# Hybrid attention and retention trunk: one transfer per row tile, rotation read from PSUM, queries and keys written to their final tiles, outputs kept in the gate tiles

## The chip, the core and the metric

The kernel runs on one core of one Trainium2 chip. A core has a matrix engine (TensorE, PE in the profile; PEld is its weight load), VectorE (DVE), ScalarE (ACT) and GpSimd (POOL), which work side by side, each through its own program, and wait for each other by semaphores. SyncE (SP) issues the transfers here; they run on 16 DMA engines. Working memory is SBUF, 128 partitions wide; matrix products land in PSUM. The metric is the device time of one execution in microseconds (us). The kernel before took 2116.13 us (median of three runs, 2115.45 to 2116.34).

## What is computed

Two layers over 2048 tokens of width 1024, then a last norm. Each layer norms its input, projects it to eight sections, runs attention over half of the width and retention over the other half, gates both, projects back and adds:

```python
def hybrid_layer(x, norm_gain, w_in, w_out, rel_bias, cos, sin):
    b, s, _ = x.shape
    hn = rms_norm(x, norm_gain)
    proj = hn @ w_in.astype(hn.dtype)
    cuts = list(np.cumsum(SPLIT_WIDTHS)[:-1])
    aq, ak, av, ag, rq, rk, rv, rg = jnp.split(proj, cuts, axis=-1)
...
    y = jnp.concatenate([ya * jax.nn.silu(ag.astype(jnp.float32)),
                         yr * jax.nn.silu(rg.astype(jnp.float32))], axis=-1).astype(x.dtype)
    return x + y @ w_out.astype(x.dtype)

def apply_rotary(t, cos, sin):
    t1, t2 = jnp.split(t, 2, axis=-1)
...
    return jnp.concatenate([t1 * c - t2 * s, t1 * s + t2 * c], axis=-1)
```

Attention has 8 heads of 64; each chunk of 64 tokens sees itself and the 8 chunks before it, with a learned bias by distance. Retention has 4 heads of 128: its queries and keys are turned by `apply_rotary`, a decaying state goes from chunk to chunk, and each head's output is normed. All inputs are float32.

## The kernel before

Every float32 operand of a matrix product is held as two fp16 parts, an upper one and a rest, and each product is made of three (upper by upper, rest by upper, upper by rest). A rest costs an operation of its own: ACT copies the upper part, and DVE subtracts it from the source.

The normed input lies transposed in `hTh` and `hTl` (L215), one pair for each stripe of 512 tokens. It gets there by row tiles of 128 tokens: `rows_hi` and `rows_lo` (L225 to L233) write the two halves, and `transpose_rows` (L235) turns each with a DMA transpose of its own. A row pair takes its two tiles from the tags `sc` and `pq`, which attention uses too.

For each layer, a loop goes over four groups `s` (two attention heads and one retention head each) and, within, over four stripes `n`. A stripe's dense work is 24 rounds of eight matmuls:

- `dense_T` (L608): sections j = 0 to 3 are attention queries, attention keys, retention queries and retention keys, three rounds each, into a PSUM tile of which there are two. `evacuate` (L627) then copies. The queries go through ACT (L631) and DVE (L634) into `qq`, and four transfers put both halves of both heads on all partitions of `st.q`. The keys go through L645 and L648 into `kk`, and four transfers place them in `st.k`. The retention sections are copied to SBUF (L662), two transfers swap the partition halves into `swp`, and DVE multiplies by the cosine table, multiplies the swapped copy by the sine table, and adds (L670). ACT and DVE then split the result (L673, L676), and keys are transposed to token order.
- `dense_V` (L738): for four token tiles a, the values of both heads, the retention values `rv` and the gate `gt`. ACT makes the upper parts and the gate's tanh (L760 to L763), DVE the rests (L766 to L770). The gate's pool has five buffers.

While PE does these rounds for one stripe, the attention and retention of the stripe before run between them. `attention` (L778) has eight units of a token tile and a head, three rounds each: PE makes the scores S (L800, L801), DVE adds the bias and takes the maximum (L804), ACT the exponential and its upper part (L807, L809), POOL the rest (L810), a DMA transpose turns the weights into `pT` (L812), and a unit later PE multiplies them with the values (L820 to L822). `out_` (L824) scales by the row sum and the gate into `ya`, and one transfer per token tile writes `y_d` in DRAM. `retention` (L866) makes dT (DVE mask L875, ACT L860, DVE rest L864), then the output and the state's update; `fin` (L911) scales by the norm and the gate into `yr`, and a second transfer goes to `y_d`.

After a layer's four groups, `wout` takes the 16 token tiles: it loads `y_d`, scales it into fp16 halves, transposes them (`y_turn`, L954; into the buffers of `tabc`, `tabs`, `qq` and `swp`) and multiplies by the output weights; `residual` adds the input and makes the next layer's rows.

PE, ACT, DVE and POOL run in the order in which the program is written. `later(k, fn)` puts a step k rounds off, and `tick` (once a round) issues what is due. The order of SP's transfers is chosen by a scheduler, and by hand only in the prologue. `push` and `pull` spread the preparation of weights over the rounds. The trigonometric tables are made by `tables` (L83) for each stripe, written to `tab_d` in eight transfers and loaded per stripe by `tab_load` (L613).

## Time and profile before

| | us |
|---|---|
| median of three runs | 2116.13 |
| the profiled execution's span | 2120.7 |
| PE busy in it | 2014.2 |
| DVE busy | 1341.8 |
| ACT busy | 1136.9 |
| POOL busy | 432.8 |

The profile is one execution, its span 4.6 us above the median. It shows each engine's busy time and what ended each idle stretch. In a group's row stand line, engine, operation, output and inputs by name, shapes and number, then busy time, mean nanoseconds of one, and the idle time ahead with what ended it. In the timeline a row has its start and length in us; brackets hold the idle time just before it and its releaser. Rows of SPq are the issue of a transfer, not its flight. A row of waits has the total, the number and the longest. In the transfers' rows the last number is the median from issue to landing.

The execution has a prologue up to about 90 us (norms of the first tokens, weights, tables, the first dense rounds), the 16 stripe rounds of layer 0 up to about 890, the output projection of layer 0 up to about 1110, the same for layer 1, and the last projection from about 1930.

### The profile page before, as it was taken

Reading aid. Unit: us, or ns where it says so; the run is one execution under the profiler, and the core shown is the slowest. Engines: PE = TensorE matmul, PEld = TensorE weight load, DVE = VectorE, ACT = ScalarE, POOL = GpSimd, SP = SyncE. Lnnn points to the kernel's source line nnn. Section 1 sums busy time; section 2 is a strip of 40 time slices with the busy share of each in tenths; the row PEclk is TensorE's granted clock in tenths of the full one; section 3 lists DMA queues with packets and bytes.
Section 4 is the critical chain, followed back from the end, with each engine's and each line's share of the span. In section 5 each row is a group of like instructions: output and inputs, shape, how many; then the busy total and the mean of one; then the engine's idle time right before and its main releaser. Section 6 shows DMA issues by size and latency. Waiting matters only on the chain.

```text
span 2120.7 us, 39351 instructions
## 1 busy us (share of the span) xinstructions
PE 2014.2 (95%) x14014; PEld 1052.9 (50%) x14014; DVE 1341.8 (63%) x4031; ACT 1136.9 (54%) x2522; POOL 432.8 (20%) x509
## 2 busy tenths in 40 slices
PE   6788999999999999988999999999999999998998
PEld 4334455555555555444444555555555555554543
DVE  7667666666656666566654666566666566666643
ACT  7455565556565554554544546554655665445432
POOL 1112221222122212221000222222222222222200
PEclk9989999999999999999999999999999999999999
DMA  8757675557476765689865556655666866648864
GB/s 247 173 111 162 138 157 119 115 110 156 109 166 133 157 164 100 120 189 254 219 179 123 119 100 135 130 119 100 140 129 123 172 152 157 124 101 176 217 193 127
DMA packets 645702, 313.63 MB, mean 148 GB/s; under 512 B 459233, under 2 KB 602081, under 8 KB 645505
## 3 DMA queue, kind: packets, MB, share of 16 engines
q1 hardware_dynamic: 645504, 311.12, 66.4%
q8 instruction: 109, 1.79, 0.4%
q14 instruction: 89, 0.72, 0.1%
HBM read 123.26 MB, written 41.98 MB: 78 GB/s over the span
## 4 chain that ended last, share of the span: by engine, by line
PE 50%; DMA 8%; DVE 5%; ACT 5%; issue 1%; SPq 1%; POOL 0%; POOLq 0%; DVEq 0%; ACTq 0%
PE dT L731 16%; PE dV L752 15%; PE dO L1093 12%; DMA pT<-pq 3%; PE r L856 2%; PE S L800 2%; PE S L801 2%; DVE sc L804 1%; DMA toep<-rel_d 1%; DMA swp<-rot 1%; PE o L820 1%; ACT pq L809 1%; PE o L821 1%; PE o L822 1%; ACT sc L807 1%
## 5 line engine op out<-in xcount | busy, mean ns | idle before, releaser
L807 ACT ACTIVATE sc<-sc,mq,cT 128x640 f32<-128x640 f32 (+4 forms) x256 | 218.4, 853 | 657.3 <-DVE mq L806 341.5
L810 POOL TENSOR_TENSOR pq<-sc,pq 128x640 f16<-128x640 f32 (+4 forms) x256 | 322.6, 1260 | 1201.7 <-ACT pq L809 610.3
L731 PE MATMUL dT<-hTh,whT 128*128 128x512 f16 x1008 | 350.2, 383 | 13.4 <-DMA hTh<-hTl 9.8
L752 PE MATMUL dV<-whV,hTh 128*128 128x512 f16 x1024 | 355.3, 383 | 4.1 <-DVE gt L770 4.1
L752 PE MATMUL dV<-wlV,hTh 128*128 128x512 f16 x1024 | 353.8, 381 | 0.0
L752 PE MATMUL dV<-whV,hTl 128*128 128x512 f16 x1024 | 353.7, 381 | 0.0
L731 PE MATMUL dT<-hTh,wlT 128*128 128x512 f16 x1008 | 347.0, 379 | 0.0
L731 PE MATMUL dT<-hTl,whT 128*128 128x512 f16 x1008 | 346.8, 379 | 0.0
L752 PEld LDWEIGHTS <-hTh 128*128 128x128 f16 x2048 | 197.5, 99 | 222.9 <-issue 8.2
L731 PEld LDWEIGHTS <-whT 128*128 128x128 f16 x2016 | 192.9, 98 | 225.8 <-issue 23.1
L804 DVE CUSTOM_DVE_ANT_0 sc<-S,bias 128x640 f32<-128x640 f32 (+4 forms) x256 | 188.6, 737 | 79.9 <-PE S L801 69.0
L1093 PE MATMUL dO<-whO,yhy 128*128 128x512 f16 x512 | 195.0, 381 | 1.1 <-DMA yhy<-rhy 1.1
L1093 PE MATMUL dO<-whO,yly 128*128 128x512 f16 x512 | 194.8, 381 | 1.1 <-DMA yly<-rly 1.1
L1093 PE MATMUL dO<-wlO,yhy 128*128 128x512 f16 x512 | 194.6, 380 | 0.0
L809 ACT ACTIVATE pq<-sc 128x640 f16<-128x640 f32 (+4 forms) x256 | 171.5, 670 | 12.5 <-DMA pT<-pq 4.6
L1093 PEld LDWEIGHTS <-yhy 128*128 128x128 f16 x1024 | 100.0, 98 | 116.7 <-DMA yhy<-rhy 1.9
L752 PEld LDWEIGHTS <-hTl 128*128 128x128 f16 x1024 | 99.5, 98 | 110.5 <-issue 2.6
L731 PEld LDWEIGHTS <-wlT 128*128 128x128 f16 x1008 | 97.6, 98 | 109.0 <-issue 1.8
L800 PE MATMUL S<-k,q 128*128 128x128 f16 (+3 forms) x592 | 143.7, 269 | 5.7 <-DVE mq L804 5.6
L820 PE MATMUL o<-v,pT 128*128 128x65 f16 x1120 | 130.2, 194 | 14.6 <-DMA pT<-pq 14.6
L820 PEld LDWEIGHTS <-pT 128*128 128x128 f16 x1120 | 105.6, 97 | 52.5 <-DMA pT<-pq 24.4
L801 PE MATMUL S<-k,q 128*128 128x128 f16 (+3 forms) x592 | 131.2, 270 | 0.0
(350 smaller groups left out, 3354.4 us busy)
## 6 DMA issues: line engine op xcount, KB each, us to landing
q<-qq SPq DMA_DIRECT2D x128, 128.0 KB, 2.5
yyy<-y_d SPq DMA_DIRECT2D x32, 512.0 KB, 4.6
stT<-in_w_in_dram SPq DMA_DIRECT2D x27, 512.0 KB, 5.0
stV<-in_w_in_dram SPq DMA_DIRECT2D x26, 512.0 KB, 4.5
k<-kk SPq DMA_DIRECT2D x128, 64.0 KB, 2.1
swp<-rot SPq DMA_DIRECT2D x64, 128.0 KB, 2.6
tabc<-tab SPq DMA_DIRECT2D x32, 256.0 KB, 2.7
tabs<-tab SPq DMA_DIRECT2D x32, 256.0 KB, 2.8
```

Source lines behind the costliest of these rows:

```text
L731: pe.matmul(ps, w_[:, j, kt, :], h_[:, kt, :], start=(m == 0), stop=(m == 23))
L752: pe.matmul(ps, h_[:, kt, a * P:(a + 1) * P], w_[:, kt, :], start=(m == 0), stop=(m == 23))
L800: pe.matmul(o, st.q[:, hx, 0, cs], k_, start=True, stop=False)
L801: pe.matmul(o, st.q[:, hx, 1, cs], k_, start=False, stop=True)
L804: dve.tensor_tensor_reduce(out=v, in0=S[:, 0:w], in1=g.bias[hx][:, 640 - w:640], scale=1.0, scalar=-3.0e38, op0=ALU.add, op1=ALU.max, accu ...
L807: act.activation(v, v, AF.Exp, bias=m[:, 0:1], scale=g.c[:, 0:1])
L809: act.activation(pq[:, 0:w], v, AF.Copy)
L810: pool.tensor_tensor(pq[:, w:2 * w], v, pq[:, 0:w], op=ALU.subtract)
L820: pe.matmul(o[:, 0:65], u.p[:, b, :], v_[:, 0:65], start=(b == 0), stop=False)
L821: pe.matmul(o[:, 0:64], u.p[:, b, :], v_[:, 65:129], start=False, stop=False)
L856: pe.matmul(out_, w_, m_, start=(i == 0), stop=(i + 1 == len(pairs)))
L1093: pe.matmul(ps, h_[:, kt, :], w_[:, kt, :], start=(m == 0), stop=(m == 23))
```

## The change

- The two fp16 halves of a row tile lie side by side in one tile, and one transpose turns both into one tile `hT`. The last token tile of `wout` keeps two transposes.
- Scores and weights of an attention unit share one tile `spq` (two buffers), as do row pairs and the scratch of the first tables.
- Tables are written in four transfers, without a negated sine, and loaded with one.
- Queries: ACT and DVE write each head's half straight into `st.q`, and two transfers copy it to the other partitions. Keys: ACT and DVE write `st.k` in place, the rest onto the opposite partitions, with no transfer.
- Rotation: DVE reads the PSUM tile itself, once times cosine and twice, by halves of 64 partitions and onto the opposite half, times plus or minus sine, then adds. There is no copy to SBUF and no swap transfer. The PSUM tile is read until one round after the first product. The steps follow one round apart, and the key's token transpose keeps its distance.
- The three outputs of a token tile are written over the gate they are multiplied with; when the third is there (`finished`), one transfer writes them to `y_d`.
- `y_turn` uses the buffers of `tab` and of the rotation's scratch, tag `qk`.

The order of PE's and POOL's instructions stays the same. The DMA issues on SP fall from 1297 to 795.

```diff
-    tab_d = [dp.tile([2, P, 512], F32, tag=f"tab{n}", name=f"tab{n}") for n in range(NS)]
+    tab_d = [dp.tile([P, 2, 512], F32, tag=f"tab{n}", name=f"tab{n}") for n in range(NS)]
...
-        dve.tensor_scalar(ang, r, -1.0, None, op0=ALU.mult)
...
+        cs_ = wk[:, 512:1024].rearrange("p (a c) -> p a c", a=2)
+        for h in range(2):
+            for hf in range(2):
+                sp.dma_start(tab_d[n][h * 64:h * 64 + 64, :, hf * 256:hf * 256 + 256], cs_[hf * 64:hf * 64 + 64])
...
     def hT_of(l, n):
         if (l, n) not in hT:
-            hT[l, n] = (hp.tile([P, KT, 512], F16, tag="hTh", name=f"hTh{l}_{n}"),
-                        hp.tile([P, KT, 512], F16, tag="hTl", name=f"hTl{l}_{n}"))
+            h_ = hp.tile([P, 2 * KT, 512], F16, tag="hT", name=f"hT{l}_{n}")
+            hT[l, n] = (h_[:, 0:KT], h_[:, KT:2 * KT], h_)
         return hT[l, n]
 
+    def halves_of(rows):
+        return rows[:, 0:D], rows[:, D:2 * D], rows
+
     def row_pair(nm):
-        return (b2.tile([P, 1280], F16, tag="sc", name=f"rh{nm}")[:, 0:D],
-                b2.tile([P, 1280], F16, tag="pq", name=f"rl{nm}")[:, 0:D])
+        return halves_of(b2.tile([P, 2560], F16, tag="spq", name=f"rw{nm}")[:, 0:2 * D])
...
-    def transpose_rows(rows, dh, dl):
-        sp.dma_start_transpose(out=dh, in_=rows[0])
-        sp.dma_start_transpose(out=dl, in_=rows[1])
+    def transpose_rows(rows, dst):
+        sp.dma_start_transpose(out=dst, in_=rows[2])
...
-        st.tabc = b1.tile([P, 512], F32, tag="tabc", name=f"tabc{nm}")
-        st.tabs = b1.tile([P, 512], F32, tag="tabs", name=f"tabs{nm}")
+        st.tab = b1.tile([P, 2, 512], F32, tag="tab", name=f"tab{nm}")
         def tab_load():
             while n not in tab_done:
                 pull(1)
-            sp.dma_start(st.tabc, tab_d[n][0])
-            sp.dma_start(st.tabs, tab_d[n][1])
+            sp.dma_start(st.tab, tab_d[n])
...
         def evacuate(j, ps):
             if j == 0:
                 st.q = b2.tile([P, 2, 2, 512], F16, tag="q", name=f"q{nm}")
-                qq = b1.tile([P, 2, 512], F16, tag="qq", name=f"qq{nm}")
-                act.activation(qq[:, 0, :], ps, AF.Copy, scale=2.0 ** -16)
+                for hx in range(2):
+                    hs = slice(hx * 64, hx * 64 + 64)
+                    act.activation(st.q[hs, hx, 0], ps[hs], AF.Copy, scale=2.0 ** -16)
 
                 def q_rest():
-                    dve.scalar_tensor_tensor(out=qq[:, 1, :], in0=ps, scalar=2.0 ** -16, in1=qq[:, 0, :], op0=ALU.mult,
-                                             op1=ALU.subtract)
                     for hx in range(2):
-                        for half in range(2):
-                            sp.dma_start(st.q[half * 64:half * 64 + 64, hx], qq[hx * 64:hx * 64 + 64])
+                        hs, os = slice(hx * 64, hx * 64 + 64), slice(64 - hx * 64, 128 - hx * 64)
+                        dve.scalar_tensor_tensor(out=st.q[hs, hx, 1], in0=ps[hs], scalar=2.0 ** -16, in1=st.q[hs, hx, 0],
+                                                 op0=ALU.mult, op1=ALU.subtract)
+                        sp.dma_start(st.q[os, hx], st.q[hs, hx])
 
                 soon(q_rest)
             elif j == 1:
                 st.k = b3.tile([P, 2, 512], F16, tag="k", name=f"k{nm}")
-                kk = b1.tile([P, 2, 512], F16, tag="swp", name=f"kk{nm}")
-                kh, kl = kk[:, 0, :], kk[:, 1, :]
-                act.activation(kh, ps, AF.Copy, scale=2.0 ** -16)
+                for hx in range(2):
+                    hs = slice(hx * 64, hx * 64 + 64)
+                    act.activation(st.k[hs, hx], ps[hs], AF.Copy, scale=2.0 ** -16)
 
                 def k_rest():
-                    dve.scalar_tensor_tensor(out=kl, in0=ps, scalar=2.0 ** -16, in1=kh, op0=ALU.mult, op1=ALU.subtract)
-                    sp.dma_start(st.k[0:64, 0, :], kh[0:64, :])
-                    sp.dma_start(st.k[64:128, 1, :], kh[64:128, :])
-                    sp.dma_start(st.k[64:128, 0, :], kl[0:64, :])
-                    sp.dma_start(st.k[0:64, 1, :], kl[64:128, :])
+                    for hx in range(2):
+                        hs, os = slice(hx * 64, hx * 64 + 64), slice(64 - hx * 64, 128 - hx * 64)
+                        dve.scalar_tensor_tensor(out=st.k[os, hx], in0=ps[hs], scalar=2.0 ** -16, in1=st.k[hs, hx],
+                                                 op0=ALU.mult, op1=ALU.subtract)
 
                 soon(k_rest)
             else:
...
+                rot = b2.tile([P, 5 - j, 512], F16, tag=f"rot{j}", name=f"rot{nm}_{j}")
                 if j == 2:
                     st.rq = rot
-                    swap()
+                    st.tmp = b1.tile([P, 2, 2, 512], F16, tag="qk", name=f"tmp{nm}")
                     if first:
                         later(1, tab_load)
                 else:
                     st.rk = rot
-                    later(8 if first else 2, swap)
+                f32 = lambda t_: t_.rearrange("p a c -> p (a c)").bitcast(F32)
+                own = f32(rot[:, 1:3]) if j == 2 else f32(st.tmp[:, 0])
+                other = f32(st.tmp[:, 1])
+
+                def cosine():
+                    dve.scalar_tensor_tensor(out=own, in0=ps, scalar=2.0 ** -16, in1=st.tab[:, 0], op0=ALU.mult,
+                                             op1=ALU.mult)
+
+                def sine(half):
+                    i_, o_ = slice((1 - half) * 64, (2 - half) * 64), slice(half * 64, half * 64 + 64)
+                    dve.scalar_tensor_tensor(out=other[o_], in0=ps[i_], scalar=(half * 2 - 1) * 2.0 ** -16, in1=st.tab[i_, 1],
+                                             op0=ALU.mult, op1=ALU.mult)
+
+                def tokens():
+                    st.kt = b1.tile([P, KT, P], F16, tag="ktok", name=f"kt{nm}")
+                    sp.dma_start_transpose(out=st.kt, in_=rot.rearrange("p a c -> p (a c)"))
+
+                d = 2 * j if first else 1
+                later(d, cosine)
+                later(d, lambda: sine(0))
+                later(d + 1, lambda: sine(1))
+                later(d + 2, lambda: dve.tensor_tensor(own, own, other, op=ALU.add))
+                later(d + 3, lambda: act.activation(rot[:, 0], own, AF.Copy))
+                later(d + 4, lambda: dve.tensor_tensor(rot[:, 1], own, rot[:, 0], op=ALU.subtract))
+                if j == 2:
+                    later(d + 5, lambda: act.activation(rot[:, 2], rot[:, 0], AF.Copy, scale=2.0 ** -11))
+                else:
+                    later(d + 5 if first else d + 12, tokens)
...
-        ya = {}
+        left = [3] * 4
+
+        def finished(a):
+            left[a] -= 1
+            if left[a] == 0:
+                t = 4 * n + a
+                sp.dma_start(y_d[t].rearrange("p (a s c) -> p a s c", a=2, c=P)[:, :, s],
+                             st.g[a].rearrange("p (a c) -> p a c", a=2))
...
-            v = b2.tile([P, 640], F32, tag="sc", name=f"sc{u.nm}")[:, 0:w]
+            spq = b2.tile([P, 2560], F16, tag="spq", name=f"spq{u.nm}")
+            v, pq = spq[:, 0:1280].bitcast(F32)[:, 0:w], spq[:, 1280:2560]
             m = b2.tile([P, 1], F32, tag="mq", name=f"mq{u.nm}")
             dve.tensor_tensor_reduce(out=v, in0=S[:, 0:w], in1=g.bias[hx][:, 640 - w:640], scale=1.0, scalar=-3.0e38,
                                      op0=ALU.add, op1=ALU.max, accum_out=m)
             dve.tensor_scalar(m, m, g.nc[:, 0:1], LN_PSC, op0=ALU.mult, op1=ALU.add)
             act.activation(v, v, AF.Exp, bias=m[:, 0:1], scale=g.c[:, 0:1])
-            pq = b2.tile([P, 1280], F16, tag="pq", name=f"pq{u.nm}")
             act.activation(pq[:, 0:w], v, AF.Copy)
             pool.tensor_tensor(pq[:, w:2 * w], v, pq[:, 0:w], op=ALU.subtract)
...
-                if u.hx == 0:
-                    ya[u.a] = b2.tile([P, P], F32, tag="ya", name=f"ya{u.nm}")
-                y = ya[u.a]
-                vs = slice(u.hx * 64, u.hx * 64 + 64)
-                dve.scalar_tensor_tensor(out=y[:, vs], in0=o[:, 0:64], scalar=rl[:, 0:1], in1=st.g[u.a][:, vs],
-                                         op0=ALU.mult, op1=ALU.mult)
-                if u.hx == 1:
-                    sp.dma_start(y_d[t][:, s * P:(s + 1) * P], y)
+                y = st.g[u.a][:, u.hx * 64:u.hx * 64 + 64]
+                dve.scalar_tensor_tensor(out=y, in0=o[:, 0:64], scalar=rl[:, 0:1], in1=y, op0=ALU.mult, op1=ALU.mult)
+                finished(u.a)
...
             def fin(t=t, a=a, r2=r2, ss=ss, nm=nm):
-                y = b1.tile([P, P], F32, tag="yr", name=f"yr{nm}")
-                dve.scalar_tensor_tensor(out=y, in0=r2[:, 0:P], scalar=ss[:, 0:1], in1=st.g[a][:, P:256],
-                                         op0=ALU.mult, op1=ALU.mult)
-                sp.dma_start(y_d[t][:, 512 + s * P:512 + (s + 1) * P], y)
+                y = st.g[a][:, P:256]
+                dve.scalar_tensor_tensor(out=y, in0=r2[:, 0:P], scalar=ss[:, 0:1], in1=y, op0=ALU.mult, op1=ALU.mult)
+                finished(a)
...
     def y_turn(u):
         if u.t + 1 == NT:
             u.h, u.lo = (b2.tile([P, 10, P], F16, tag="pT", name=f"y{c}{u.nm}")[:, 0:KT, :] for c in "hl")
+            sp.dma_start_transpose(out=u.h, in_=u.rows[0])
+            sp.dma_start_transpose(out=u.lo, in_=u.rows[1])
         else:
-            u.h = b1.tile([P, KT, P], F16, tag=("tabc", "qq")[u.t % 2], name=f"yh{u.nm}")
-            u.lo = b1.tile([P, KT, P], F16, tag=("tabs", "swp")[u.t % 2], name=f"yl{u.nm}")
-        transpose_rows(u.rows, u.h, u.lo)
+            yT = b1.tile([P, 2 * KT, P], F16, tag=("tab", "qk")[u.t % 2], name=f"yT{u.nm}")
+            u.h, u.lo = yT[:, 0:KT], yT[:, KT:2 * KT]
+            transpose_rows(u.rows, yT)
...
```

More of the change, by code (lines that the diff above doesn't have):

```diff
@@ L83, in tables @@
     def tables(n, wk):
-        ang, k, r, k2 = wk
+        ang, k, k2, r = (wk[:, i * 256:(i + 1) * 256] for i in range(4))
         pi = k2.bitcast(I32)
@@ L266, in hi @@
         def hi(self):
-            if self.rows:
-                self.rw = (self.rows[:, 0:D], self.rows[:, D:2 * D])
+            if self.rows is not None:
+                self.rw = halves_of(self.rows)
                 act.activation(self.rw[0], self.x, AF.Copy)
@@ L274, in lo @@
         def lo(self):
-            if self.rows:
+            if self.rows is not None:
                 dve.tensor_tensor(self.rw[1], self.x, self.rw[0], op=ALU.subtract)
@@ L987, in mul @@
         def mul():
-            u.x = xt if on_pe or rows else psS.tile([P, D], F32, tag="S", name=f"xn{nm}")
+            u.x = xt if on_pe or rows is not None else psS.tile([P, D], F32, tag="S", name=f"xn{nm}")
             dve.scalar_tensor_tensor(out=u.x, in0=xt, scalar=u.rs[:, 0:1], in1=gains[l].b, op0=ALU.mult, op1=ALU.mult)
@@ L999, in upper @@
             else:
-                u.rows = rows or row_pair(nm)
+                u.rows = halves_of(rows) if rows is not None else row_pair(nm)
                 rows_hi(u.rows, u.x)
@@ L1180, in dma @@
         def dma(k):
-            transpose_rows(us[k].rows, *us[k].h)
+            transpose_rows(us[k].rows, us[k].h[2])
         us = []
@@ L1261, in hybrid_trunk @@
     sp.dma_start(invf_sb, invf)
-    t0 = tables(0, [gp.tile([P, 256], F32, tag="gt", name=f"wk{i}") for i in range(4)])
+    t0 = tables(0, b2.tile([P, 2560], F16, tag="spq", name="wk").bitcast(F32)[:, 0:1024])
     go_on(t0)
@@ L1328, in V_un @@
         next(vu[0])
-    t1 = tables(1, [xs0[1][:, i * 256:(i + 1) * 256] for i in range(4)])
+    t1 = tables(1, xs0[1])
     steps = {"d": lambda: go_on(d0), "t": lambda: go_on(t0), "u": lambda: go_on(t1), "r": lambda: go_on(rl_),
@@ L1380, in hybrid_trunk @@
                     push(norms_from_input(range(4 * n + 4, 4 * n + 8), late[0:4] if n == 1 else None,
-                                          tables(n + 1, [xs0[n + 1][:, i * 256:(i + 1) * 256] for i in range(4)])), 21)
+                                          tables(n + 1, xs0[n + 1])), 21)
                 if (l, s, n) == (0, 1, 1):
```

69 lines of the change are left out of this document (15 added, 54 removed).

## Prediction

> **What bounds the kernel now.** I read the page's head first, then the busy time stage by stage, then what TensorE (PE) waits for, last the timeline around the longest stalls.
>
> ```profile
> span 2120.7 us, 39351 instructions
> PE 2014.2 (95%) x14014; PEld 1052.9 (50%) x14014; DVE 1341.8 (63%) x4031; ACT 1136.9 (54%) x2522; POOL 432.8 (20%) x509
> 45.00:90.00 45.00, 35.19 (x160) 15.63 (x158) 29.35 (x70) 23.49 (x52) 3.35 (x10) 0.89 0.79 180
> 90.00:215.00 125.00, 102.43 (x664) 51.46 (x663) 84.95 (x235) 66.14 (x143) 27.00 (x32) 0.91 0.66 139
> 300.00:865.00 565.00, 556.84 (x4127) 296.68 (x4126) 366.83 (x1183) 316.34 (x748) 135.49 (x153) 1.00 0.63 133
> 865.00:1010.00 145.00, 126.84 (x851) 64.45 (x850) 90.48 (x253) 76.16 (x146) 27.44 (x28) 0.96 0.89 199
> 1112.00:1890.00 778.00, 767.09 (x5565) 405.80 (x5564) 492.78 (x1551) 427.12 (x1008) 176.27 (x202) 1.00 0.62 129
> 1890.00:2000.00 110.00, 103.01 (x759) 54.12 (x756) 75.06 (x216) 59.70 (x119) 26.66 (x27) 0.98 0.79 182
> ```
>
> PE is the bound: 2014.2 of 2120.7 us. The change leaves its instructions and their order as they are, so all that can be gained is idle time, 106.5 us, and time lost to a lower clock. The rows by stage (length, then busy time of PE, PE's loads, DVE, ACT and POOL, then granted clock) place the idle time: 9.8 us in 45 to 90, 22.6 in 90 to 215, 18.2 in 865 to 1010, 7.0 in 1890 to 2000. The two long steady stretches hold 8.2 and 10.9 in 1343 us; there a shorter wait can bring almost nothing.
>
> ```profile
> PE r L856 <- DVE dT L864: 20.5, 16, 5.1
> PE S L800 <- DVE mq L804: 5.6, 2, 2.9
> DVE rot L670 <- DMA swp<-rot: 60.1, 26, 6.2
> 106.76 0.69 DVE L670 TENSOR_TENSOR rot<-rot,tabc 128x512 f32<-128x512 f32 x1 [2.90 <-DMA swp<-rot]
> 110.43 0.29 PE L856 MATMUL r<-rv,dT 128*128 128x128 f16 x1 [5.07 <-DVE dT L864]
> 729.72 0.68 DVE L670 TENSOR_TENSOR raw<-raw,tabc 128x512 f32<-128x512 f32 x1
> 730.65 0.23 PE L856 MATMUL r<-rv,dT 128*128 128x128 f16 x1 [1.51 <-DVE dT L864]
> ```
>
> A row of waits gives total, number and longest. DVE stands 60.1 us for swap transfers of the rotation, PE only 20.5 for DVE's rest of dT. The two touch where a rotation multiply stands just ahead of that rest in DVE's program order: at 106.76 behind a swap wait, at 729.72 as plain work.
>
> **The change part by part.**
>
> *Row transposes, prologue.* PE's longest stall:
>
> ```profile
> 63.69 1.22 DVE L276 TENSOR_TENSOR hTl<-hTl,hTl 128x1024 f16<-128x1024 f32 x1
> 64.24 3.23 SPq L237 DMA_TRANSPOSE hTl<-hTh  x1
> 72.67 1.56 SPq L236 DMA_TRANSPOSE hTh<-hTl  x1
> 74.32 3.10 SPq L237 DMA_TRANSPOSE hTl<-hTl  x1
> 78.61 3.57 PE L731 MATMUL dT<-hTh,whT 128*128 128x512 f16 x8 [9.81 <-DMA hTh<-hTl]
> 145.24 1.89 PE L731 MATMUL dT<-hTh,whT 128*128 128x512 f16 x8
> 209.96 3.57 PE L731 MATMUL dT<-hTh,whT 128*128 128x512 f16 x8 [3.62 <-DMA hTh<-rhn]
> pT<-pq SPq DMA_TRANSPOSE x256, 3.4
> yhy<-rhy SPq DMA_TRANSPOSE x32, 3.2
> ```
>
> The rows are ready when DVE ends at 64.91, yet SP sends their second half only at 74.32, because the queue ahead is full (two transposes a tile, two swaps, x loads). With one transpose a tile and no swaps, SP is free by then; DVE's own added work (below, 2.8 us) makes the rows ready at about 67.7. A transpose of 16 blocks is not in the trace: 8 blocks land in 3.2 us and 10 in 3.4, so by that slope 16 take 4.0; bounds are 3.2 (no slower) and 6.4 (two of 8 in a row). Landing at 71.7, and PE is there at 68.80: a stall of 2.9 instead of 9.81, **−6.9**. After both DMA stalls here the first eight matmuls took 3.57 us against 1.89, so such a stall costs 1.7 more. I keep that cost here and drop it at 209.96, where one transfer for two and fewer issues ahead should end most of the 3.62: **−3 −1.7**.
>
> By the Trainium skill, "TensorE: Matmul & The Clock Gate", "Why this matters for your kernels", PE gaps over about 3 us bring the clock down; both rows agree, and by that rule the prologue's dip goes if its stall ends below 3.
>
> *Rotation.* Per stripe and group (32 of them) two evacuations and four swap transfers go, and each rotation's four DVE operations become five.
>
> ```profile
> L634 DVE SCALAR_TENSOR_TENSOR qq<-dT,qq 128x512 f16<-128x512 f32 x32 | 21.9, 683 | 13.2 <-ACT qq L631 13.2
> L670 DVE TENSOR_TENSOR rot<-rot,tabc 128x512 f32<-128x512 f32 x32 | 27.9, 871 | 68.3 <-DMA swp<-rot 60.1 <-DMA y_d<-yr 8.1
> L631 ACT ACTIVATE qq<-dT 128x512 f16<-128x512 f32 x32 | 18.8, 587 | 9.8 <-PE dT L731 9.5 <-PE dT L712 0.3
> 1204.86 0.28 DVE L864 SCALAR_TENSOR_TENSOR dT<-dT,r 128x128 f16<-128x128 f16 x1
> 1205.98 0.22 PE L856 MATMUL r<-rv,dT 128*128 128x128 f16 x1
> ```
>
> Halves of 64 partitions have the same 512 elements a partition, so I price each at 0.683, as L634, which reads PSUM as they do; bounds: half of that (fewer partitions) and 0.871. Queries and keys add one such operation each, so DVE gets 4 × 0.683 = 2.7 us a stripe, 88 us in all, against the 60.1 of swap waits that go. ACT stays even: two halves more, two evacuations fewer. What was late behind a swap goes: in 90 to 215 the 5.07 and some 2 us of the smaller stalls, **−7**. In the steady stretches, at stalls like 730.65, the multiply stood ahead of the rest and now comes three rounds earlier. Of the 20.5 us of PE's waits on that rest, six such places hold 0.6 to 1.5 each: **−6**. The cover fails at the retention unit in q's round: its rest ends 0.84 us before PE asks (1205.14 to 1205.98), while DVE now has one operation of 0.68 more ahead of it and may wait 0.59 for ACT's second half. That lacks 0.4; in about half of the stripes the slack is several us instead. Bounds 0 and 32 × 1.3 = 42; I take **+5**. The PSUM tile is held one round longer, within the three rounds until PE needs it: nothing.
>
> The Trainium skill, "VectorE: DVE Perf Modes", "Two Vector instructions with no wait between them", speaks against the change: an instruction whose start quadrant differs from its predecessor's is held until all earlier ones have finished. No row of before has such halves. At an estimated 0.08 us each (the overlap of neighbouring rows here) and some 11 holds a stripe it would be 28 us more of DVE, and by it the sum would end about 3 us higher.
>
> *Queries, keys, tables.* Six q and k transfers a stripe and one table load go from SP; the key transfers (2.1 us to landing) aren't what PE waits for, so beside SP's room this is worth nothing.
>
> *One tile for scores and weights.* DVE's next-but-one reduction now waits for the transpose's landing, not ACT's copy alone.
>
> ```profile
> 592.10 1.25 SPq L812 DMA_TRANSPOSE pT<-pq  x1
> 597.91 0.81 DVE L804 CUSTOM_DVE_ANT_0 sc<-S,bias 128x640 f32<-128x640 f32 x1
> ```
>
> Issue 592.10 plus 3.4 is 595.5, 2.4 before that reduction: a little only in the slow transfers, **+1** (bounds 0 and 21: one transfer in twelve, of 256, late by 1 us).
>
> *Outputs in gate tiles.* The gate tile is free only when its transfer has landed. The last piece written and its transfer now, and ACT's next write:
>
> ```profile
> 1242.97 0.28 DVE L832 SCALAR_TENSOR_TENSOR ya<-o,rl,gt 128x64 f32<-128x64 f32 x1
> 1243.28 0.32 SPq L835 DMA_DIRECT2D y_d<-ya  x1
> 1245.21 0.47 ACT L761 ACTIVATE gt<-dV,ughV 128x256 f32<-128x256 f32 x1
> y_d<-ya SPq DMA_DIRECT2D x128, 64.0 KB, 2.1
> 1242.76 0.92 ACT L807 ACTIVATE sc<-sc,mq,cT 128x640 f32<-128x640 f32 x1 [2.50 <-DVE rl L826]
> ```
>
> Of five buffers, the one that the stripe's fourth token tile takes was used by the third tile of the stripe before. Landing at 1243.28 + 2.1 = 1245.4, 0.2 after ACT starts to write it: ACT will wait once a stripe, by an estimate of 0.7 us (0.2 here, twice or more where SP is behind). Queued behind are the value's evacuations, then DVE's rests of the same tile. ACT idles 2.50 before its next exp, so most is taken up: **+4**, bounds 0 and 31 × 1.5 = 47.
>
> *Transitions (865 to 1010, 1890 to 2000).*
>
> ```profile
> 883.01 1.80 SPq L236 DMA_TRANSPOSE yhy<-rhy  x1
> 887.56 0.82 DVE L804 CUSTOM_DVE_ANT_0 sc<-S,bias 128x640 f32<-128x640 f32 x1 [4.63 <-DMA yhy<-rhy]
> 888.44 0.27 PE L800 MATMUL S<-k,q 128*128 128x128 f16 x1 [2.88 <-DVE mq L804]
> 889.96 1.23 SPq L237 DMA_TRANSPOSE yly<-rly  x1
> ```
>
> The output rows share buffers with the scores; their second transpose waits until the last rotation has released its table tile. PE loses 5.6 us at two such places and about as much in smaller stalls behind them. Now one transpose goes out, into a tile that the rotation leaves rounds earlier. The wait itself, the 16 blocks, stays partly. I take **−10**, and 1.7 for a dip: **−1.7**; bounds 0 and −25.2.
>
> Sum: −6.9 −3 −1.7 −7 −6 −10 −1.7 = −36.3; +5 +1 +4 = +10; net −26. The profiled execution spans 2120.7, 4.6 above the median of 2116.1: 2094.4 by its own time, **2090** for the median.
>
> **The rivals.**
>
> *Little changes.* DVE's 88 us take the place of the swap waits, so the retention rests come as late as before, and outside the prologue only half of the transitions' gain stays: −6.9 −5 +10 gives −2, about **2114**. For it: 729.72 to 730.65 is work, not a wait. Against it: those two late units lose an operation ahead of them.
>
> *Slower: the gate transfer.* If landing sets ACT's write of the fourth gate tile in every stripe, ACT's delay passes to DVE's rests and on to PE. From 36 + 4 − 10 = 30 us over 31 stripes, 1.0 us a stripe reaching PE cancels the gain; at 2 us it is +62 − 30 = +32, **2148**; at 1.5, 2133. Against it stand the 2.50 us of idle ACT.
>
> *A larger gain.* If the idle time from 45 to 215 falls to a quarter and the transitions' to a third, 24 + 17 + 6 us go, with an estimated 8 for the clock (0.89 to 0.98 in those stages), less 10: **2071**.
>
> **How the numbers follow.** The forecast 0.60 (own range 2077 to 2104), larger gain 0.12, little change 0.14, slower 0.14. Half of the little-change case lies within 0.2% (4.2 us, about what a measurement can tell). Faster 0.60 + 0.12 + 0.05 = 0.77, same 0.08, slower 0.15. The range 2070 to 2124 leaves 0.06 below and 0.13 above.
>
> **What would show it.** Prologue: a first dT stall near 3 us. Rotation: no DVE wait on swaps, retention rests at or before their places, and PE's waits on dT under 10 us. Gates: ACT waits on the output transfer under 1 us a stripe. Transitions: no stall of PE for L804's scores above 2 us. I am wrong if the steady stretches' idle time grows, or if ACT or DVE ends PE's waits more often than now.

## The result and the profile after

The changed kernel takes 2191.9 us (median of four runs, 2191.0 to 2193.7) against 2115.8 for the kernel before on the same chip: a ratio of 1.036, with a 95% interval of 1.0345 to 1.0375. It is 76 us slower where 26 us less were forecast.

The head of the page and the busy time by stage, as they were shown of before (length, PE, PE's loads, DVE, ACT and POOL, then PE's granted clock, share of the DMA engines and GB/s):

```profile
span 2190.0 us, 38235 instructions
PE 2032.0 (93%) x14014; PEld 1053.5 (48%) x14014; DVE 1444.4 (66%) x4155; ACT 1145.8 (52%) x2522; POOL 429.2 (20%) x509
45.00:90.00 45.00, 41.33 (x189) 18.19 (x188) 34.79 (x78) 27.60 (x58) 3.77 (x11) 0.94 0.67 167
90.00:215.00 125.00, 100.87 (x654) 50.38 (x653) 88.90 (x235) 63.37 (x137) 26.08 (x31) 0.92 0.57 121
300.00:880.00 580.00, 558.94 (x4090) 295.51 (x4088) 403.01 (x1228) 319.44 (x747) 132.13 (x151) 0.99 0.50 110
880.00:1020.00 140.00, 114.39 (x809) 58.06 (x807) 83.57 (x227) 66.54 (x131) 30.02 (x29) 0.96 0.73 161
1145.00:1945.00 800.00, 773.01 (x5577) 406.27 (x5576) 542.83 (x1620) 433.76 (x1013) 175.19 (x203) 1.00 0.48 106
1945.00:2065.00 120.00, 100.41 (x718) 51.99 (x717) 72.60 (x202) 54.50 (x110) 25.60 (x27) 0.94 0.64 147
```

The span is 69.3 us longer than before's: PE is busy 17.8 us longer with the same instructions, and idle 51.5 us longer (2190.0 − 2032.0 = 158.0 against 106.5). The mean granted clock went from 0.987 to 0.985, which by these rounded figures is some 4 of the 17.8; where the others come from is not traced. Of these stages only the prologue gained: 45 to 90 has 3.7 us of idle time, where before had 9.8. The two steady stretches now hold 21.1 and 27.0 us of idle time, where before held 8.2 and 10.9. DVE is busy 102.6 us longer.

The changed kernel's waits (total, number, longest):

```profile
DVE v L751 <- ACT rv L747: 185.0, 79, 8.1
ACT gt L746 <- DMA y_d<-gt: 37.6, 24, 6.0
DVE k L648 <- ACT k L643: 48.1, 23, 2.6
DVE spq L797 <- DMA pT<-spq: 24.7, 14, 3.9
PE r L842 <- DVE dT L850: 35.6, 38, 2.5
PE S L792 <- ACT fj L200: 7.5, 3, 3.4
```

PE's wait for DVE's rest of dT went from 20.5 us in 16 places to 35.6 in 38: shorter than the old 5.1 each, but more than twice as many. Of the first three rows, the one on the output transfer is new; before, the first had 108.3 us and the third 39.2. No wait on a swap is left.

### The profile page after: what moved, and what is told of

It is laid out like the page before. It is cut to its first block, busy times and chain, and to the rows that moved or that the text cites. A ratio compares the mean times of both kernels' runs of the same rounds, so it can differ in the third digit from the quotient of the medians.

```text
span 2190.0 us, 38235 instructions
## 1 busy us (share of the span) xinstructions
PE 2032.0 (93%) x14014; PEld 1053.5 (48%) x14014; DVE 1444.4 (66%) x4155; ACT 1145.8 (52%) x2522; POOL 429.2 (20%) x509
## 5 line engine op out<-in xcount | busy, mean ns | idle before, releaser
L800 ACT ACTIVATE spq<-spq,mq,cT 128x640 f32<-128x640 f32 (+4 forms) x256 | 218.5, 853 | 731.7 <-issue 419.1
L737 PE MATMUL dV<-whV,hT 128*128 128x512 f16 x2048 | 584.1, 382 | 15.5 <-DVE tmp L671 8.4
L716 PE MATMUL dT<-hT,whT 128*128 128x512 f16 x2016 | 582.6, 383 | 6.8 <-DMA hT<-rwn 3.3
L802 POOL TENSOR_TENSOR spq<-spq 128x640 f16<-128x640 f32 (+4 forms) x256 | 320.1, 1250 | 1298.5 <-ACT spq L801 672.4
L737 PEld LDWEIGHTS <-hT 128*128 128x128 f16 x3072 | 293.5, 98 | 345.5 <-issue 17.4
L737 PE MATMUL dV<-wlV,hT 128*128 128x512 f16 x1024 | 352.4, 380 | 0.0
L716 PE MATMUL dT<-hT,wlT 128*128 128x512 f16 x1008 | 347.2, 380 | 0.0
L1080 PE MATMUL dO<-whO,yTy 128*128 128x512 f16 x960 | 296.0, 387 | 11.7 <-DVE gt L755 7.4
L797 DVE CUSTOM_DVE_ANT_0 spq<-S,bias 128x640 f32<-128x640 f32 (+4 forms) x256 | 188.3, 735 | 54.3 <-DMA pT<-spq 24.7
L1080 PE MATMUL dO<-wlO,yTy 128*128 128x512 f16 x480 | 185.7, 387 | 1.5 <-DVE wlO L332 1.5
L751 DVE SCALAR_TENSOR_TENSOR v<-dV,v 128x128 f16<-128x128 f32 x128 | 36.9, 289 | 188.3 <-ACT rv L747 185.0
```

What stands on the lines that cost most here:

```text
L716: pe.matmul(ps, w_[:, j, kt, :], h_[:, kt, :], start=(m == 0), stop=(m == 23))
L737: pe.matmul(ps, h_[:, kt, a * P:(a + 1) * P], w_[:, kt, :], start=(m == 0), stop=(m == 23))
L797: dve.tensor_tensor_reduce(out=v, in0=S[:, 0:w], in1=g.bias[hx][:, 640 - w:640], scale=1.0, scalar=-3.0e38, op0=ALU.add, op1=ALU.max, accu ...
L800: act.activation(v, v, AF.Exp, bias=m[:, 0:1], scale=g.c[:, 0:1])
L802: pool.tensor_tensor(pq[:, w:2 * w], v, pq[:, 0:w], op=ALU.subtract)
L1080: pe.matmul(ps, h_[:, kt, :], w_[:, kt, :], start=(m == 0), stop=(m == 23))
```

## The experiments

All ratios are to the kernel before, run on the same chip in the same set of runs.

| version | ratio (95% interval) |
|---|---|
| changed kernel | 1.036 (1.0345 to 1.0375) |
| own output tiles | 1.0202 (1.0178 to 1.0226) |
| rotation by swaps | 1.0278 (1.0257 to 1.0298) |
| queries, keys by transfers | 1.0225 (1.0205 to 1.0245) |
| these three together | 1.0046 (1.0028 to 1.0065) |
| six gate buffers | 1.0246 (1.0231 to 1.0262) |
| scores and weights in two tiles | 1.0247 (1.0224 to 1.0270) |
| one ScalarE operation each, two VectorE halves | 1.0324 (1.0306 to 1.0342) |
| only the joined input transposes | 0.9919 (0.9902 to 0.9935) |
| the same, with the change's rotation | 1.0003 (0.9993 to 1.0013) |
| queries, keys by transfers, rests twice | 1.0325 (1.0306 to 1.0343) |
| second sine half a round earlier | 1.0334 (1.0318 to 1.0351) |
| only the joined input transposes, outputs in six gate buffers | 0.9906 (0.9888 to 0.9924) |
| only the joined input transposes, PSUM tile held | 0.9925 (0.9908 to 0.9942) |
| only the joined input transposes, last subtraction twice | 0.9993 (0.9982 to 1.0004) |

### One part undone at a time

**Own output tiles.**

```diff
-                y = st.g[u.a][:, u.hx * 64:u.hx * 64 + 64]
-                dve.scalar_tensor_tensor(out=y, in0=o[:, 0:64], scalar=rl[:, 0:1], in1=y, op0=ALU.mult, op1=ALU.mult)
-                finished(u.a)
+                if u.hx == 0:
+                    ya[u.a] = b2.tile([P, P], F32, tag="ya", name=f"ya{u.nm}")
...
+                    sp.dma_start(y_d[t][:, s * P:(s + 1) * P], y)
```

> The changed kernel with the outputs in tiles of their own again (two transfers a token tile), all else as changed. In the changed kernel's trace ScalarE waits 37.6 us (24 times, longest 6.0) for the output transfer before it writes a gate tile. Theory G (the gate tile that is free only when its transfer has landed is the main cost): most of the 76 us loss comes back, about 2115 to 2145. Theory R (the rotation's longer VectorE work read from PSUM is the main cost): nearly nothing, 2180 to 2195. Theory S (the shared tile of scores and weights is the main cost): 2175 to 2195.

**Rotation by swaps**, in all stripes but the first and the last of a layer:

```diff
+                if not direct:
+                    act.activation(own, ps, AF.Copy, scale=2.0 ** -16)
+                def swap():
+                    sp.dma_start(other[0:64, :], own[64:128, :])
+                    sp.dma_start(other[64:128, :], own[0:64, :])
```

> The changed kernel with the rotation by copies to SBUF and swap transfers again in every stripe but the first and the last of a layer. Theory R (VectorE's two more operations a stripe, and the PSUM tile held two rounds): 2120 to 2150. Theory G: 2180 to 2195. Theory S: 2180 to 2200.

**Queries and keys by transfers**: one ACT and one DVE operation each into scratch, eight transfers.

```diff
+                kh, kl = st.tmp[:, 1, 0, :], st.tmp[:, 1, 1, :]
+                act.activation(kh, ps, AF.Copy, scale=2.0 ** -16)
...
+                    sp.dma_start(st.k[0:64, 0, :], kh[0:64, :])
```

> The changed kernel with queries and keys copied by one ScalarE and one VectorE operation each and placed by eight transfers again. By theory Q (each half copy costs as much as a whole one, and VectorE starts only behind both: 1.2 us more of ScalarE and 1.4 us of VectorE a stripe): 2150 to 2170. Theories R, G and S: 2175 to 2200.

**The three together** hold all these edits.

> The three edits above undone together: of the change only the joined transposes, the shared tile of scores and weights, and the joined tables stay. If theory S holds, it stays near 2175 to 2190; if R, G or Q or their sum holds, it falls to 2095 to 2120, and the joined transposes' gain at the prologue (7 us) shows.

Measured: 2163.1, 2178.1, 2166.7 and 2128.7 us, on a chip where before took 2119.7. Each version's distance from the changed kernel's ratio, times 2116 us, is what its part costs: the outputs 33 us (1.0360 − 1.0202), the rotation 17, queries and keys 29; together 79, and undoing all three at once brings 66. None of the theories alone holds; the costs add up, with some overlap. The last version is still 10 us slower than before, which the three parts can't explain.

### What each part's cost consists of

**Six gate buffers.**

```diff
-            gt = gp.tile([P, 256], F32, tag="gt", name=f"gt{nm}_{a}")
+            gt = gp.tile([P, 256], F32, tag="gt", bufs=6, name=f"gt{nm}_{a}")
```

> The changed kernel with six gate buffers in place of five, nothing else. The buffer that a stripe's fourth token tile takes then was used two tiles earlier and has been free for over 10 us. If the wait for the landed transfer is what the outputs in place cost (33 us, from the run with own output tiles), this brings 2155 to 2170 and ScalarE's 37.6 us of waits on that transfer go to nearly nothing. If it is the order of SP's queue, the 512-byte pieces or the writes in place, it stays at 2180 to 2195.

It brings back 24 of the outputs' 33 us, with the outputs still written in place. ACT's wait on the output transfer is gone from its waits, and DVE's wait behind it falls from 185.0 us to:

```profile
DVE v L751 <- ACT rv L747: 147.0, 80, 4.3
```

So for these 24 us the mechanism is the landing: ACT waits to write the gate, and DVE's rests, in order behind it, wait for ACT. What the other 9 of the 33 are in the changed kernel stays open.

**Scores and weights in two tiles**, output rows turned by two transposes again:

```diff
-            spq = b2.tile([P, 2560], F16, tag="spq", name=f"spq{u.nm}")
-            v, pq = spq[:, 0:1280].bitcast(F32)[:, 0:w], spq[:, 1280:2560]
+            v = b2.tile([P, 640], F32, tag="sc", name=f"sc{u.nm}")[:, 0:w]
...
+            pq = b2.tile([P, 1280], F16, tag="pq", name=f"pq{u.nm}")
```

> The changed kernel with scores and weights in two tiles again, and the output projection's row pairs turned by two transposes again; input rows keep the one transpose. In all four runs so far the last projection is some 14 us longer than before, with VectorE's score reduction waiting for the weights' transpose. If the shared tile is the cause: 10 to 20 us less than the changed kernel, 2172 to 2182, nearly all of it in the two projections. If the joined transposes pay there: 2190 to 2205. If the shared tile also delays the steady stripes: under 2170.

It brings 24 us. The two edits were undone together, so the run alone doesn't part the shared tile from the joined transposes of the output rows; the rows below speak for the tile. Where the time comes back is seen in POOL's rows: the first and last rest of weights in the last stripe's attention, which runs inside the last projection. First the changed kernel's timeline, then this version's:

```profile
1999.47 1.40 POOL L802 TENSOR_TENSOR spq<-spq 128x640 f16<-128x640 f32 x1 [11.81 <-ACT spq L801]
...
2058.56 1.40 POOL L802 TENSOR_TENSOR spq<-spq 128x640 f16<-128x640 f32 x1 [5.36 <-ACT spq L801]
```

```profile
1986.32 1.40 POOL L807 TENSOR_TENSOR pq<-sc,pq 128x640 f16<-128x640 f32 x1 [9.66 <-ACT pq L806]
...
2032.22 1.40 POOL L807 TENSOR_TENSOR pq<-sc,pq 128x640 f16<-128x640 f32 x1 [3.44 <-ACT pq L806]
```

The eight units take 59.1 us there against 45.9. The same kind of stretch in the changed kernel's timeline shows why:

```profile
2010.29 2.03 SPq L233 DMA_TRANSPOSE yTy<-rwy  x1
2012.49 0.82 DVE L797 CUSTOM_DVE_ANT_0 spq<-S,bias 128x640 f32<-128x640 f32 x1 [2.39 <-DMA pT<-spq]
2016.43 0.48 PE L792 MATMUL S<-k,q 128*128 128x384 f16 x1 [3.42 <-ACT fj L200]
```

While the projection runs, its row pairs take turns with the attention units in the same two buffers. A unit's score reduction then waits for a transpose of the unit just before, not of one two units back. ACT's exponential and square stand behind it, and PE waits for the square, because it writes the PSUM tile that the next scores take.

**One ScalarE operation each, two VectorE halves.**

```diff
-                for hx in range(2):
-                    hs = slice(hx * 64, hx * 64 + 64)
-                    act.activation(st.k[hs, hx], ps[hs], AF.Copy, scale=2.0 ** -16)
+                kh = st.tmp[:, 1, 0, :]
+                act.activation(kh, ps, AF.Copy, scale=2.0 ** -16)
...
+                        sp.dma_start(st.k[hs, hx], kh[hs])
```

> The changed kernel with the upper parts of queries and keys made by one ScalarE operation each and placed by transfers; VectorE keeps its two half operations each. It splits the 29 us that queries and keys cost. If ScalarE's second operation and VectorE's wait behind it are the cost: 2160 to 2172. If VectorE's second operation is: 2182 to 2192. Half and half: 2172 to 2182.

It brings back 8 of the 29 us: the other 21 lie with VectorE's second operations.

**Queries and keys by transfers, each rest issued twice.**

```diff
                     dve.scalar_tensor_tensor(out=kl, in0=ps, scalar=2.0 ** -16, in1=kh, op0=ALU.mult, op1=ALU.subtract)
+                    dve.scalar_tensor_tensor(out=kl, in0=ps, scalar=2.0 ** -16, in1=kh, op0=ALU.mult, op1=ALU.subtract)
```

> The version with queries and keys by copies and transfers (ratio 1.0225), with each of VectorE's two whole rests issued twice (the second writes the same values again): 0.683 us more for each of them, 44 us of VectorE in all, no halves of 64 partitions, no wait for a second ScalarE operation. If VectorE's plain time at these places is what the halves cost: the ratio of the run with VectorE halves and single ScalarE operations, 1.030 to 1.035. If it is the halves as such (held instructions, opposite partitions): 1.022 to 1.027.

1.0325 against 1.0324: two more whole operations a stripe cost just what the two halves' extra operations cost. Within the intervals (some 4 us to either side) it is VectorE's plain time.

### The joined transposes alone, and the rotation on top

**Only the joined input transposes**: the three parts undone, scores and weights in two tiles, output rows by two transposes. The joined trigonometric tables stay too, and the last stripe of a layer keeps the change's rotation.

> Only the joined transposes of the input rows stay (prologue, first stripes, next layer's rows) with the joined tables: outputs in own tiles, queries, keys and rotation through copies and transfers, scores and weights in two tiles, output rows by two transposes. If the prologue's gain is real and everything else cost: 2100 to 2112, faster than both. If one tile for both halves of the input costs elsewhere: 2113 to 2122.

2095.4 us on a chip where before took 2113.8: faster than both kernels. What each of the parts that stay gains was not run by itself. Its page and the stage from 45 to 90:

```profile
span 2091.4 us, 39205 instructions
PE 2007.9 (96%) x14014; PEld 1051.1 (50%) x14014; DVE 1350.5 (65%) x4033; ACT 1132.8 (54%) x2516; POOL 434.1 (21%) x511
45.00:90.00 45.00, 40.75 (x204) 18.77 (x203) 36.65 (x90) 27.46 (x60) 5.21 (x13) 1.00 0.76 184
```

**The same with the outputs in the gate tiles, and six buffers for them** (the edits as above):

> The fastest version so far (0.992) with the outputs in the gate tiles as in the change (one transfer per token tile), but six gate buffers. If the outputs in place are harmless once no buffer is waited for: 0.989 to 0.993. If they cost by themselves (9 us lay between own tiles and six buffers in the changed kernel): 0.995 to 0.998.

0.9906: in this version the outputs are harmless, in place and with one transfer, once no buffer is waited for. This is the fastest version of the study, 2094.7 us where before took 2114.8; its interval overlaps that of the version with own tiles.

**The change's rotation on the version with the joined input transposes:**

> The rotation of the change alone on the fastest version so far (0.992 of before): read from PSUM, three products from it, no swap transfers; all else as in that version. If the rotation's cost is its own (17 us in the changed kernel): ratio to before 0.998 to 1.003. If it costs only because other parts have used up VectorE's slack: 0.990 to 0.995. If the swap waits that go are worth what was forecast (a gain of 8): 0.987 to 0.990.

1.0003 against 0.9919: the rotation costs 18 us by itself, as in the changed kernel. Its page and a wait:

```profile
span 2115.0 us, 38931 instructions
PE 2012.5 (95%) x14014; PEld 1051.0 (50%) x14014; DVE 1394.5 (66%) x4091; ACT 1100.0 (52%) x2458; POOL 428.1 (20%) x509
PE dV L741 <- DVE tmp L675: 11.0, 14, 2.7
```

DVE is busy 44.0 us longer than without it. The 52.3 us of waits for swaps that the version without it has are gone, but DVE's wait for ACT's `rv` copy has grown from 108.7 to 147.3 us. PE's 11.0 us of waits for the sine product, the last reader of the PSUM tile, left two explanations: VectorE's longer work, or the PSUM tile that is held longer. Three runs bear on them.

**Second sine half a round earlier**, in the changed kernel:

```diff
-                later(d + 1, lambda: sine(1))
+                later(d, lambda: sine(1))
```

> The changed kernel with the second half of the sine product one round earlier, so that the PSUM tile is released a round earlier. In the changed kernel TensorE waits 8.4 us for that product at value rounds. If holding the PSUM tile is the rotation's cost: 8 to 12 us less, 2178 to 2184. If VectorE's time is: no change or a little more, as the retention rests then stand behind two more products: 2188 to 2198.

**PSUM tile held** by a read of one column, without the operations, and **last subtraction twice**, without the hold, both in the version with the joined input transposes:

```diff
+                    later(2, lambda: dve.tensor_copy(warm, ps[:, 0:1]))
```

> The fastest version's rotation (ratio 0.992), with one added read by VectorE of a single column of the PSUM tile two rounds after its copy: the tile is held as long as the change holds it, at 0.1 to 0.2 us of VectorE each. If the held tile is what the rotation costs alone (18 us, and TensorE waited 11 us for it there): 0.996 to 1.000. If VectorE's time is: 0.992 to 0.994.

```diff
                 later(d + 4, lambda: dve.tensor_tensor(rot[:, 1], own, rot[:, 0], op=ALU.subtract))
+                later(d + 4, lambda: dve.tensor_tensor(rot[:, 1], own, rot[:, 0], op=ALU.subtract))
```

> The fastest version with the rotation's last subtraction issued twice (the second writes the same values): two VectorE operations of 0.7 to 1.1 us more per stripe, as many as the rotation of the change adds, and no PSUM tile held. If VectorE's time is what the rotation costs: 0.997 to 1.001. If the held tile is: 0.992 to 0.995.

In the last one the second subtraction writes the same values for the keys only; for the queries the source lies in the tile that the first has written, so that part is not the reference's. The operations' shapes and engines are as stated.

The earlier sine half brings 5.5 us (1.0360 − 1.0334, with intervals that still overlap a little); PE's waits for the sine product, 8.4 us in the changed kernel, are gone with it. Holding the tile costs nothing measurable (0.9925 against 0.9919). The two subtractions cost 16 us (0.9993 against 0.9919), nearly the rotation's 18. Its page:

```profile
span 2114.3 us, 39273 instructions
PE 2011.9 (95%) x14014; PEld 1051.0 (50%) x14014; DVE 1391.7 (66%) x4097; ACT 1134.1 (54%) x2516; POOL 436.9 (21%) x511
```

41.2 us more of VectorE, 22.9 us more of span than in the page above; that was another chip, and the ratio's 16 us is the fairer figure.

The equal totals support VectorE's time as the cost, but don't show it by themselves, since the two versions lose at different places. With the two subtractions, PE waits 25.8 us for the rest of dT (18.1 without them); with the change's rotation 16.3, but 11.0 for the sine product and 13.5 (6.7) for ACT's half of dT. From POOL's first rest of weights in the first stripe to that in the third, the rotation loses 5.4 us and the subtractions 1.1. The held tile was tested without VectorE's added work ahead of its last read; that this work costs by releasing the tile late is not excluded. The run with the earlier sine half puts such a share at some 5 us in the changed kernel.

### Where VectorE's time turns into span

Two stretches of before, each cut at the same work in the changed kernel (from POOL's first rest of weights of one stripe to that of another). Before, then the change:

```profile
1202.00:1303.00 101.00, 101.00 (x783) 55.14 (x782) 67.98 (x200) 54.58 (x127) 27.26 (x26) 1.00 0.57 112
1567.00:1778.00 211.00, 206.85 (x1536) 109.69 (x1535) 136.18 (x451) 125.51 (x297) 49.76 (x57) 1.00 0.69 146
```

```profile
1239.00:1340.00 101.00, 100.59 (x779) 54.85 (x778) 72.94 (x209) 54.71 (x125) 26.77 (x26) 1.00 0.46 91
1609.00:1830.00 221.00, 208.41 (x1530) 109.75 (x1529) 148.85 (x464) 125.49 (x291) 49.37 (x56) 0.99 0.53 120
```

In the first, two stripes long, DVE goes from 67% to 72% of the stretch and nothing is lost. In the second, four stripes long, DVE goes from 65% to 67%, and 10 us are lost. Before the change ACT is at 59% there, against 54% in the first: in one of these stripes it goes over the output weights for their maxima, and DVE waits for it in turn. The changed kernel's waits, over the whole execution:

```profile
DVE omaxO L505 <- ACT stO0m L308: 9.4, 7, 3.3
DVE omaxO L505 <- ACT stO1m L308: 8.8, 7, 3.0
```

The kernel before has these waits too (8.2 and 8.1 us), so they mark the stretch but aren't what grew. In the second stretch DVE's wait for `rv` grew from 12.0 to 22.2 us, and 5.1 us of ACT's waits for the output transfer are new; in the first the wait for `rv` grew from 7.2 to 10.4. DVE's share of the time doesn't tell the two stretches apart. That the waits between the engines do is a reading of these rows, which no run tested.

## Why the prediction was wrong

**The prologue** was right on its long stall. The 9.81 us are gone; what stands there now is shorter than the 2.9 forecast, and has another cause:

```profile
42.40 0.16 PE L1225 MATMUL ms<-mbV,ones 128*128 128x2 bf16 x1 [2.40 <-DVE mbV L1219]
69.40 0.61 PE L737 MATMUL dV<-whV,hT 128*128 128x512 f16 x2 [2.69 <-DVE gt L755]
69.84 0.38 PE L737 MATMUL dV<-wlV,hT 128*128 128x512 f16 x1
71.60 0.63 PE L737 MATMUL dV<-wlV,hT 128*128 128x512 f16 x1
hT<-rwn SPq DMA_TRANSPOSE x14, 4.4
```

The transpose of 16 blocks lands in 4.4 us, forecast 4.0 by a slope from one group of 8 blocks (3.2); before, the groups of 8 blocks landed in 3.2 to 4.8, those of these rows in 4.1 and 3.2. The clock cost of the first stall, which was kept in the sum, stays in the changed kernel: behind the stall of 2.69 the granted clock is 0.66 from 70 to 75, and a matmul of 0.38 us takes 0.63. At 42.40 PE now stalls 2.40 us, where before it stalled 0.83, and the clock is 0.82 from 45 to 50. In the version with the joined input transposes the whole stage from 45 to 90 has a clock of 1.00, with a longest stall of 2.70; before, it had 0.89. So the length of the stall does not decide this alone. The Trainium skill's limit of about 3 us ("TensorE: Matmul & The Clock Gate", "Why this matters for your kernels") agrees with that version, but not with the changed kernel, where stalls of 2.40 and 2.69 cost clock; the measurement decides. Only half of the −6.9 reaches the stripes: POOL's first rest of weights comes at 80.66 against 84.11 before, and at 77.19 in the version with the joined input transposes.

**The stall at 209.96** stayed, with its clock cost (−4.7 in the sum, 0.3 measured):

```profile
209.48 3.57 PE L716 MATMUL dT<-hT,whT 128*128 128x512 f16 x8 [3.34 <-DMA hT<-rwn]
```

Its issue was not what came late. The rows are ready at 204.06 and their transpose is issued at 204.58, where before had 204.26 and 204.60 for the first of its two; and it was that first one, `hTh`, which PE's wait of before named.

**The rotation is the step that failed first.** "What was late behind a swap goes" was worth −13 in the sum, and the added operations +5; measured, the whole is +18. The swap waits, 60.1 us of DVE, were not on PE's path so far as the runs show: where they go, nothing is gained, and DVE's wait for `rv` is longer. At the stall of 5.07 that was put down to one, the changed kernel shows:

```profile
102.54 0.29 PE L842 MATMUL r<-rv,dT 128*128 128x128 f16 x2 [2.53 <-ACT dT L846]
105.33 0.29 PE L842 MATMUL r<-rv,dT 128*128 128x128 f16 x1 [2.35 <-DVE dT L850]
```

These are 4.88 us in one unit; before, its two waits were 1.95 and 5.07. With the change's rotation alone they are 5.64 and 2.09, against 5.00 without it. ACT and DVE are late there with the first stripes' norms and tables, and now with the rotation's products among them, so the swap wait mostly stood in time that was lost anyway. The added operations were priced by the one unit whose slack was looked at. The 88 us more of VectorE that were forecast, rotation, queries and keys together, cost 17 + 21 = 38 us, about two fifths of themselves. The rival "little changes" named this mechanism, DVE's work in the swap waits' place, but took all its price from the same +5.

**Queries and keys** were priced with these operations and "worth nothing" else. ScalarE's second operation, with the wait behind it, cost 8 us more.

**The shared tile** was sized +1, from its slack in a steady stripe (2.4 us at one reduction). There it held: from POOL's first rest of the first layer's third stripe round to that of its fifteenth, the two-tile version takes 659.5 us against the changed kernel's 655.3; in the second layer, from the first round to the fifteenth, 747.5 against 747.2. The projections, where row pairs take every other buffer, weren't looked at, and by single traces nearly all of the 24 us lie there: 13.2 by the rows above, and 9.5 more in the first layer's (243.2 us against 233.7 from POOL's first rest of the stripe that runs into it to that of the next). The transitions' −11.7 drowned in it. The version with the joined input transposes, which keeps the change's rotation in those stripes, gains 11.9 us there against before (5.2, 1.9 and 4.8, by the same rests).

**The gate tiles**: the mechanism was right, the size wrong. The wait at the fourth token tile was put at 0.7 us a stripe, taken up by ACT's idle time, +4. ACT waited 1.6 us in the mean of 24 places, and 24 us came back with a sixth buffer, some 0.8 us a stripe. The rival "slower" had the right side and this mechanism, but needed 1.0 us a stripe to cancel the gain and priced up to 2; the landing by itself is a third of the loss.

The sum by the runs: the version with the joined input transposes −17 (0.9919), rotation +17, queries and keys +29, outputs +33, shared tile +24, together +86 against +76 measured. The difference is put down to overlap, parts that are late in the same stripe and share the loss; the three parts undone at once (66 against 79) show that there is some.

**The Trainium skill's held instruction** (the rule of "VectorE: DVE Perf Modes", "Two Vector instructions with no wait between them", weighed in the prediction) shows in the rows of the changed kernel, though not in the time:

```profile
620.60 0.69 DVE L671 SCALAR_TENSOR_TENSOR tmp<-dT,tab 64x512 f32<-64x512 f32 x1
621.33 0.35 DVE L899 SCALAR_TENSOR_TENSOR gt<-r,rss,gt 128x128 f32<-128x128 f32 x1
621.60 0.28 DVE L850 SCALAR_TENSOR_TENSOR dT<-dT,r 128x128 f16<-128x128 f16 x1
```

The instruction behind the half starts 0.04 after its end, where the next neighbours overlap by 0.08, so the Trainium skill's rule agrees; all 44 rows between 300 and 880 that follow such a half without a wait start 0.01 to 0.04 after its end. The estimate of 3 us for it can't be told from nothing: halves and whole operations gave the same ratio (1.0324 and 1.0325).

## What to carry to other kernels

A wait of 60 us on an engine that isn't the bound can be worth nothing that shows, while 40 to 44 us of work added to the same engine cost 16 to 21: price added work at the stages in which the engines wait for each other, not by the mean busy share or by one unit's slack. When two tiles become one, or an output is written over an input, list every user of the buffers, also those of other phases, and what each waits for last; one more gate buffer was worth 24 us here. Undo the parts one by one before judging a change of several parts: a version that keeps little more than the joined input transposes is 0.8% faster than the kernel before, where the whole change is 3.6% slower.

## What was not expected of the hardware

Half of the partitions saves no time: VectorE's halves of 64 partitions took 0.688 us in the sine products, against 0.683 for the whole query rest of before, and ACT's halves of the query copy 0.587, as long as the whole copy of before (0.587). That was assumed in the price, but its weight wasn't: a split across partitions was a second full operation here, and it was paid in six places a stripe, on ACT and DVE.
